# Layer 0's input projection in five chunks of the contraction instead of four

## The chip, the core and the metric

The kernel runs on one core of a Trainium2 chip. The core has a matrix engine (PE, with its weight loads listed as PEld), a vector engine (DVE), an activation engine (ACT), a general engine (POOL), and a queue engine (SP) that issues nearly all transfers from the chip's memory. Each engine takes its own instructions in the order in which they were written into its queue; engines wait for each other by semaphores. Time is the device time of one launch in microseconds (us), lower is better.

## The reference, cut to what matters

Two layers of a bidirectional encoder on x of 256 positions by 2048 channels, all in float32. `c` is one vector of 2048 values.

```python
c_act = silu(c)
for l in range(2):
    shift, scale, gate = split(c_act @ w_ada[l] + b_ada[l], 3)     # w_ada[l]: 2048 x 6144
    h = rmsnorm(x, norm_g[l]) * (1 + scale) + shift                # 256 x 2048
    z = h @ w_in[l]                                                # w_in[l]: 2048 x 6656, 13 pieces of 512
    ...                                                            # four mixers on the 13 pieces:
    # Fourier (f_x, f_g), neighbourhood attention (na_q, na_k, na_v, na_g),
    # retention (r_q, r_k, r_v, r_g), convolution (cv_a, cv_b, cv_g)
    x = x + gate * (concat(o_fft, o_na, o_ret, o_cv) @ w_out[l])   # w_out[l]: 2048 x 2048
out = rmsnorm(x, final_g)
```

So `h` cannot be used before the modulation (shift and scale) of its channels is known, and that takes two thirds of `w_ada[l]`, 33.5 MB in layer 0, read through once. `w_in[l]` is 54.5 MB.

## The kernel before, in words

**Tiles.** The 2048 channels are 16 K tiles of 128. A column of the modulation for one K tile (`Ada`, line 519) is worked out on DVE: a 512 KB half row block of `w_ada` is multiplied by silu(c), spread over all partitions, and summed along the row (line 534). Each K tile takes four of these for layer 0's `h`: shift and scale, two halves each.

**A step of weights** (`Weights`, line 332) is a transfer of two K tiles of one piece of `w_in` (512 KB; one K tile, 256 KB, where a chunk has an odd tail), a split on two engines, and matmuls. The split keeps float32 accuracy with a fast matmul type: ACT writes the rounded high part `whi` (line 351), DVE the rest, `wlo` (line 353). `h` is split the same way into `hh` and `hl`. Each product is then three matmuls: hh·whi, hl·whi, hh·wlo. Pieces that are wanted with channels on the partitions (CVB, CVA, NAQ, NAK, NAG, FGP, CVG) go by lines 370 to 373 with 256 columns each, twelve matmuls per K tile; the others (FXP, NAV, RV, RQ, RK, RG) go by rows, lines 402 to 404 with 512 columns each, six matmuls per K tile. Ten pieces ("first") run in every chunk; RK, CVG and RG ("second") run once at the end over all 16 K tiles.

**Chunks.** In layer 0 the modulation is not there when the kernel starts. The K tiles are therefore cut into chunks, `CH0`, and the ten first pieces run chunk by chunk: while the matmuls of one chunk run, the `Ada` steps for the K tiles of the next chunk are loaded and summed. `merge` (line 1084) spreads these steps evenly between the weight steps of the running chunk, except its last `KEEP` = 4. After three quarters of them comes `prep_x` (line 233): DVE scales x by the reciprocal norm, PE transposes it into a PSUM bank. After the last comes `mod_cols` (line 1115; three small DVE instructions) and `prep_h` (line 282): per K tile two ACT instructions of 128x256 (`hh`, line 296, and the unrounded h, line 301) and a DVE subtraction (`hl`, line 309 or 314). `prep_h` is given a higher place in the order of every engine than the work written around it.

```python
    chunks = first_steps(0, CH0, SEED0)
    steps += mod_chunk(0, *CH0[0])
    for i in range(len(CH0) - 1):
        steps += merge(chunks[i][:-KEEP], mod_chunk(0, *CH0[i + 1])) + chunks[i][-KEEP:]
    tail = chunks[-1] + second_steps(0)
    steps += between(tail, SPAN[0], gates(0, 0) + gates(0, 1) + pair(1, 0))
```

**What a chunk costs beside its matmuls.** A piece has two PSUM banks of the four that are called "acc"; so two pieces are open at most. At the end of each chunk its sum is copied out to an SBUF tile `z` (`done`, line 456; ACT, line 471, 128x512 each, two per piece). In a later chunk the piece is either seeded, that is ACT copies z back into the bank before its first matmul (`seed`, line 437, instruction at line 442) and copies the total out again, or not seeded, and then DVE adds the bank to z (line 473). `SEED0` says for every chunk which of a piece's two banks are seeded. In the first chunk nothing is seeded. The seed of the next piece is issued after the first step of the running one (line 387).

**Order.** `FIRST` (line 1237) has the order of the ten pieces in each chunk. The order differs from chunk to chunk. The last chunk's order is written so that the mixers can start one after another: the convolution's pieces CVB and CVA come first. The mixers' work is cut into small bits which a `Pacer` (line 41) calls after each weight step at fixed rates, so the amount of mixer work that is queued between two weight steps goes by the number of steps, not by time. The tail of layer 0 (last chunk and the three second pieces) also has 48 `Ada` steps spread in it: the gates of layer 0 and the first K tiles of layer 1.

**Loads.** All weight and `Ada` loads go through SP's queue in the order of the steps. There are nine buffers of 512 KB (`RAW`) and, until nine loads ahead of the tail, two more. `whi` and `wlo` have four buffers each (`WB`): the splits may run four steps ahead of the matmuls.

Of the kernel before, what the change touches and what calls it, by code (L numbers as in the profile page):

```python
# [34 lines left out]
FXP, FGP, NAQ, NAK, NAV, NAG, RQ, RK, RV, RG, CVA, CVB, CVG = range(13)  # L35
# [56 lines left out]
def trunk(ctx, tc, x, c, cols, w_ada, w_in, w_fft, na_bias, consts, conv_w_pw, w_out, final_g, out):  # L92
# [322 lines left out]
    def held(w):  # L415

        return w.tags is None and len(ring) >= WB and any(ring[-WB] in u for u in holds)
# [630 lines left out]
    def first_steps(l, chunks, seeds):  # L1048
        groups = {p: Group(l, p, seeds) for p in FIRST[l][0]}
        res = []  # L1050
        for c, (k0, n) in enumerate(chunks):
            ws = []
            order = FIRST[l][min(c, len(FIRST[l]) - 1)]
            for p, after in zip(order, order[1:] + (None,)):
                for k, w in pieces(k0, n):
                    ws.append(Weights(in_src(l, p, k, w), groups[p], k, w, k == k0, k + w == k0 + n))
                    ws[-1].next = groups.get(after)
            res.append(ws)
        return res

    def second_steps(l):
        ws = []
        for p in SECOND[l]:
            g = Group(l, p, (0,))
            for ck in range(4):
                for k in (0, 2):
                    ws.append(Weights(in_src(l, p, 4 * ck + k), g, 4 * ck + k, 2, ck == 0 and k == 0,
                                      ck == 3 and k == 2))
                if p == SECOND[l][-1] and ck < 3:
                    ws.append(Call(o_split(ck)))  # L1070
        return ws
# [12 lines left out]
    def merge(a, b):  # L1084

        n = sum(isinstance(s, Weights) for s in a)
        res, done, i = [], 0, 0
        for s in a:
            res.append(s)
            if isinstance(s, Weights):  # L1090
                i += 1
                while done * n < i * len(b) and done < len(b):
                    res.append(b[done])
                    done += 1
        return res + b[done:]
# [28 lines left out]
    def mod_chunk(l, k0, n):  # L1124
        def done():
            mod_cols(l, k0, n)
            prep_h(l, k0, n)

        if k0 == 0:
            both = [Ada(l, which, k, h) for h in range(2) for k in range(n) for which in range(2)]  # L1130
            both[-1].then = done
            both.insert(2, Call(lambda: spread_c(1)))
            both.insert(4, Call(rms_first))
        else:
            both = mods(l, (0, 1), range(k0, k0 + n), done)
        half = len(both) // 2 if k0 == 0 else 3 * len(both) // 4
        return both[:half] + [Call(lambda: prep_x(l, k0, n))] + both[half:]
# [42 lines left out]
# [6 lines that stand above are left out]
# [27 lines left out]
    for s in steps:  # L1213
        if isinstance(s, Step):
# [3 lines left out]
            while (n_split < min(len(weights), n_w[0] + WB) and pos[id(weights[n_split])] < n_load  # L1218
                   and not held(weights[n_split]) and n_run >= 4 * CH0[0][1]):
                weights[n_split].split()  # L1220
# [8 lines left out]
        if isinstance(s, Weights):  # L1229
# [7 lines left out]
FIRST = (((CVB, FGP, NAQ, CVA, NAK, FXP, NAV, NAG, RV, RQ),  # L1237
          (NAG, NAQ, RQ, NAK, CVB, RV, FXP, FGP, NAV, CVA),
          (RV, NAK, FGP, NAV, NAG, FXP, CVA, NAQ, CVB, RQ),
          (CVB, CVA, NAQ, FXP, NAV, NAG, NAK, FGP, RV, RQ)),  # L1240
         ((NAV, CVA, RV, NAQ, FGP, RQ, NAK, FXP, CVB, NAG),
          (CVB, CVA, NAQ, NAK, NAG, FXP, NAV, RV, FGP, RQ)))
# [3 lines left out]
SECOND = ((RK, CVG, RG), (RK, CVG, RG))  # L1246
LAG = 4
B = (0, 1)
SEED0 = ((), (0, 1), (0, 1), (0, 1))
SEED1 = ((), (0, 1))  # L1250
EVAC = (0, 0)
AHEAD = 100
PACE = {'conv': (2, 1.5), 'na': (0.67, 1), 'fft': (1.75, 2.5), 'ret': (1.25, 1.5)}
CH0 = ((0, 2), (2, 3), (5, 5), (10, 6))
CH1 = ((0, 8), (8, 8))
KEEP = 4
H32A = 2
# [75 lines left out]
```

## Time and profile before

| | |
|---|---|
| median of three runs | 945.87 us (945.86, 945.87, 956.63) |
| the profiled execution, its time | 946.63 us |
| its span, first to last instruction | 944.8 us |
| PE busy | 904.1 us, 96% of the span |
| DVE busy | 774.5 us, 82% |
| ACT busy | 600.4 us, 64% |
| read from memory | 256.61 MB, 274 GB/s over the span |

The page lists groups of instructions as line, engine, operation, output <- inputs, shape, count, then the time that they were busy, the mean of one in ns, and the idle time of the engine just before them with what ended it. A table of windows gives, for each stretch of the span, the busy time of each engine with the number of instructions in it, the clock that PE was granted (1.00 is full), the share of the transfer engines' time that was in use, and GB/s. PE's matmuls overlap their neighbours, so their durations add up to more than the time they take; what one costs is the distance from its start to the next one's start. DVE and ACT instructions overlap by some 0.08 us in the same way.

### The profile page before, as it was taken

Reading aid. Unit: us, or ns where it says so; the run is one execution under the profiler, and the core shown is the slowest. Engines: PE = TensorE matmul, PEld = TensorE weight load, DVE = VectorE, ACT = ScalarE, POOL = GpSimd, SP = SyncE. Lnnn points to the kernel's source line nnn. Section 1 sums busy time; section 2 is a strip of 40 time slices with the busy share of each in tenths; the row PEclk is TensorE's granted clock in tenths of the full one; section 3 lists DMA queues with packets and bytes.
Section 4 is the critical chain, followed back from the end, with each engine's and each line's share of the span. In section 5 each row is a group of like instructions: output and inputs, shape, how many; then the busy total and the mean of one; then the engine's idle time right before and its main releaser. Section 6 shows DMA issues by size and latency. Waiting matters only on the chain.

```text
span 944.8 us, 14744 instructions
## 1 busy us (share of the span) xinstructions
PE 904.1 (96%) x5312; PEld 770.0 (81%) x5312; DVE 774.5 (82%) x1260; ACT 600.4 (64%) x1039; POOL 23.2 (2%) x35
## 2 busy tenths in 40 slices
PE   7789999999999999999999999999999999999995
PEld 3779798898977787788778999999768889788784
DVE  5988989789999999889877897559977967678962
ACT  4478966879877766544645464659889645643541
POOL 1000000000000010000000000000000001010000
PEclk7989999999999999999999999999999999999999
DMA  9999999798797778979966999777755666479922
GB/s 336 398 347 388 368 389 372 255 386 270 248 295 252 248 253 286 327 269 363 326 225 211 341 374 367 222 226 236 228 174 164 199 226 199 140 243 331 326 96 89
DMA packets 109132, 259.68 MB, mean 275 GB/s; under 512 B 8450, under 2 KB 10626, under 8 KB 108804
## 3 DMA queue, kind: packets, MB, share of 16 engines
q1 hardware_dynamic: 108004, 256.11, 78.1%
q0 software_dynamic: 768, 2.11, 0.7%
q8 instruction: 41, 0.67, 0.3%
q10 hardware_dynamic: 288, 0.52, 0.1%
q14 instruction: 31, 0.25, 0.1%
HBM read 256.61 MB, written 2.11 MB: 274 GB/s over the span
## 4 chain that ended last, share of the span: by engine, by line
PE 65%; DVE 15%; DMA 10%; ACT 5%; issue 4%; SPq 0%; POOL 0%; DVEq 0%; POOLq 0%; ACTq 0%
PE acc L402 13%; PE acc L403 13%; PE acc L404 13%; PE acc L370 6%; PE acc L372 6%; PE acc L373 6%; DMA raw<-in_w_ada_dram 5%; DVE wlo L353 5%; DVE raw L534 4%; DMA raw<-in_w_in_dram 4%; PE pwb L791 3%; ACT whi L351 2%; DVE cy L719 1%; DVE cy L703 1%; DMA wsm<-in_w_fft_dram 1%
## 5 line engine op out<-in xcount | busy, mean ns | idle before, releaser
L351 ACT ACTIVATE whi<-raw 128x1024 fp32r<-128x1024 f32 (+1 forms) x272 | 278.0, 1030 | 185.9 <-PE acc L404 81.9
L353 DVE TENSOR_TENSOR wlo<-raw,whi 128x1024 fp32r<-128x1024 f32 (+1 forms) x272 | 320.4, 1183 | 57.6 <-ACT whi L351 54.9
L534 DVE CUSTOM_DVE_ANT_0 raw<-raw,cbc 128x1024 f32<-128x1024 f32 x192 | 233.3, 1221 | 44.7 <-DMA raw<-in_w_ada_dram 44.6
L370 PE MATMUL acc<-hh,whi 128*128 128x256 f32 x896 | 254.6, 285 | 2.3 <-ACT hh L296 1.3
L373 PE MATMUL acc<-hh,wlo 128*128 128x256 f32 x896 | 251.3, 283 | 3.6 <-DVE wlo L353 3.5
L372 PE MATMUL acc<-hl,whi 128*128 128x256 f32 x896 | 252.4, 282 | 1.8 <-DVE hl L309 1.8
L402 PE MATMUL acc<-whi,hh 128*128 128x512 f32 x600 | 241.9, 405 | 5.2 <-ACT z L471 3.5
L403 PE MATMUL acc<-wlo,hh 128*128 128x512 f32 x600 | 239.0, 398 | 1.4 <-DVE wlo L353 1.3
L404 PE MATMUL acc<-whi,hl 128*128 128x512 f32 x600 | 238.2, 397 | 0.0
L370 PEld LDWEIGHTS acc<-hh,whi 128*128 128x128 f32 x896 | 170.3, 190 | 7.7 <-issue 2.8
L373 PEld LDWEIGHTS acc<-hh,wlo 128*128 128x128 f32 x896 | 169.4, 190 | 5.2 <-DVE wlo L353 5.0
L372 PEld LDWEIGHTS acc<-hl,whi 128*128 128x128 f32 x896 | 170.4, 190 | 2.7 <-DVE hl L309 2.1
L402 PEld LDWEIGHTS acc<-whi,hh 128*128 128x128 f32 x600 | 113.2, 189 | 34.8 <-ACT z L471 3.9
L403 PEld LDWEIGHTS acc<-wlo,hh 128*128 128x128 f32 x600 | 113.5, 189 | 28.9 <-DVE wlo L353 4.4
L404 PEld LDWEIGHTS acc<-whi,hl 128*128 128x128 f32 x600 | 113.4, 189 | 27.5 <-issue 1.4
L471 ACT ACTIVATE z<-acc 128x512 f32<-128x512 f32 x108 | 62.2, 599 | 29.7 <-PE acc L373 16.1
L715 ACT ACTIVATE cvp<-uT,constants 128x256 f32<-128x256 f32 x160 | 70.8, 502 | 7.8 <-DVE cy L719 7.8
L719 DVE TENSOR_TENSOR cy<-cy,cvp 128x512 f32<-128x512 f32 x80 | 52.9, 689 | 5.9 <-ACT cvp L715 5.5
L442 ACT ACTIVATE acc<-z 128x512 f32<-128x512 f32 x72 | 41.6, 601 | 0.2
L703 DVE SCALAR_TENSOR_TENSOR cy<-uT,constants,cy 128x256 f32<-128x256 f32 x80 | 34.9, 481 | 0.2
L210 ACT ACTIVATE junk<-xs 128x512 f32<-128x512 f32 x16 | 9.5, 595 | 36.8 <-DVE xs L496 36.8
L495 DVE TENSOR_TENSOR yt<-acc,gate 128x512 f32<-128x512 f32 x16 | 10.5, 685 | 13.6 <-PE acc L404 13.6
(212 smaller groups left out, 710.1 us busy)
## 6 DMA issues: line engine op xcount, KB each, us to landing
raw<-in_w_in_dram SPq DMA_DIRECT2D x198, 512.0 KB, 5.2
raw<-in_w_ada_dram SPq DMA_DIRECT2D x192, 512.0 KB, 6.0
raw<-in_w_out_dram SPq DMA_DIRECT2D x64, 512.0 KB, 5.6
raw<-in_w_in_dram SPq DMA_DIRECT2D x20, 256.0 KB, 7.4
nab<-in_na_bias_dram SPq DMA_DIRECT2D x16, 192.0 KB, 5.0
xs<-in_x_dram SPq DMA_DIRECT2D x2, 1024.0 KB, 6.0
gate<-gate_row POOLq DMA_DIRECT2D x8, 256.0 KB, 5.5
wsm<-in_w_fft_dram SPq DMA_DIRECT2D x4, 512.0 KB, 3.7
```

The lines of the kernel that those rows point to most:

```text
L351: self.on_act = A.activation(self.hi[:, :n], self.raw[:, :n], AF.Copy).ins
L353: self.on_dve = V.tensor_tensor(self.lo[:, :n], self.raw[:, :n], self.hi[:, :n].bitcast(F32), op=ALU.subtract).ins
L370: T.matmul(o, wh[:, sl], hh[:, k], start=fresh and blk % 2 == 0 and blk // 2 not in g.seeded, stop=False, skip_group_check=True)
L372: T.matmul(o, wh[:, sl], hl[:, k], start=False, stop=False, skip_group_check=True)
L373: flags["mm"] = T.matmul(o, wl[:, sl], hh[:, k], start=False, stop=en, skip_group_check=True).ins
L402: T.matmul(o, hh[:, k, sl], wh, start=st, stop=False, skip_group_check=m in g.seeded)
L403: T.matmul(o, hh[:, k, sl], wl, start=False, stop=False, skip_group_check=m in g.seeded)
L404: flags["mm"] = T.matmul(o, hl[:, k, sl], wh, start=False, stop=en, skip_group_check=m in g.seeded).ins
L471: A.activation(o, i, AF.Copy, scale=0.125 if last and self.piece == NAQ else 1.0)
L534: flags["sum"] = V.tensor_tensor_reduce(w, w, cbc[:, self.half * KH:(self.half + 1) * KH], 0.5, 0.0, ALU.mult, ALU.add, to).ins
L715: A.activation(d[:, i], uT[:, b + i, t:t + S], AF.Copy, scale=w[:, t, b + i:b + i + 1])
L719: V.tensor_tensor(y[:, b:b + 2], y[:, b:b + 2], d, op=ALU.add)
```

## The change

Layer 0's 16 K tiles are cut into five chunks of 2, 2, 3, 4 and 5 instead of four of 2, 3, 5 and 6. The new fourth chunk gets an order of the ten pieces of its own; the other orders stay with the first, second, third and last chunk. In the second chunk a piece has its first bank seeded and its second bank added by DVE; in the three later chunks both banks are seeded as before.

```diff
 FIRST = (((CVB, FGP, NAQ, CVA, NAK, FXP, NAV, NAG, RV, RQ),
           (NAG, NAQ, RQ, NAK, CVB, RV, FXP, FGP, NAV, CVA),
           (RV, NAK, FGP, NAV, NAG, FXP, CVA, NAQ, CVB, RQ),
+          (CVB, NAV, NAQ, NAK, RQ, NAG, RV, FXP, FGP, CVA),
           (CVB, CVA, NAQ, FXP, NAV, NAG, NAK, FGP, RV, RQ)),
...
-SEED0 = ((), (0, 1), (0, 1), (0, 1))
+SEED0 = ((), (0,), (0, 1), (0, 1), (0, 1))
...
-CH0 = ((0, 2), (2, 3), (5, 5), (10, 6))
+CH0 = ((0, 2), (2, 2), (4, 3), (7, 4), (11, 5))
```

A pair in `CH0` is (first K tile, number of K tiles). Work by chunk, each with ten pieces; "steps" are weight steps, "sums" the `Ada` steps for the next chunk that are merged into it:

| chunk | before: K tiles, steps, sums | after: K tiles, steps, sums |
|---|---|---|
| 0 | 2, 10, 12 | 2, 10, 8 |
| 1 | 3, 20 (10 of one K tile), 20 | 2, 10, 12 |
| 2 | 5, 30 (10 of one K tile), 24 | 3, 20 (10 of one K tile), 16 |
| 3 | 6, 30 (last chunk) | 4, 20, 20 |
| 4 | | 5, 30 (10 of one K tile; last chunk) |

## The prediction

> **What bounds the kernel now.** I read the page first: its busy times, then the slices of the span (40 of 23.6 us each).
>
> ```profile
> PE 904.1 (96%) x5312; PEld 770.0 (81%) x5312; DVE 774.5 (82%) x1260; ACT 600.4 (64%) x1039; POOL 23.2 (2%) x35
> ...
> PE   7789999999999999999999999999999999999995
> ...
> DVE  5988989789999999889877897559977967678962
> ...
> PEclk7989999999999999999999999999999999999999
> DMA  9999999798797778979966999777755666479922
> ```
>
> PE is the bound of the whole and is short of work only in the first three slices, where the transfers are full and the granted clock dips. DVE is at nine tenths in slices ten to sixteen (212 to 378 us): the tail of layer 0, which is also touched by the change. So I ask two things: what PE loses in the chunks before the tail, and whether the tail can run faster if PE has less to do in it.
>
> The windows come next. A K tile of ten pieces has 96 main matmuls (6 pieces by 12, 4 by 6), so counting them from the first one at 24.77 gives the borders of the chunks; the counts in the rows (198, 299, 493, 673) hold these and the few transposes and mixer matmuls. Rows: chunks 0, 1, 2, 3, then the second pieces up to the place where PE last waits for a split.
>
> ```profile
> 24.77:67.42 42.65, 34.91 (x198) 30.71 (x198) 38.12 (x63) 25.23 (x40) 0.00 (x0) 0.88 1.00 374
> 67.42:114.50 47.08, 44.77 (x299) 40.03 (x298) 42.18 (x69) 41.18 (x71) 0.00 (x0) 1.00 1.01 376
> 114.50:188.72 74.22, 73.47 (x493) 66.55 (x493) 62.18 (x102) 54.24 (x89) 0.00 (x0) 1.00 0.93 340
> 188.72:293.97 105.25, 102.72 (x673) 91.64 (x672) 101.11 (x180) 88.11 (x172) 1.83 (x3) 1.00 0.89 304
> 293.97:340.40 46.43, 44.60 (x253) 34.82 (x252) 44.23 (x97) 33.14 (x67) 1.11 (x2) 1.00 0.67 223
> ```
>
> A matmul's cost is the distance between starts:
>
> ```profile
> 47.38 0.39 PE L404 MATMUL acc<-whi,hl 128*128 128x512 f32 x1
> 47.61 0.39 PE L402 MATMUL acc<-whi,hh 128*128 128x512 f32 x1
> ...
> 59.74 0.28 PE L370 MATMUL acc<-hh,whi 128*128 128x256 f32 x1
> 59.86 0.28 PE L372 MATMUL acc<-hl,whi 128*128 128x256 f32 x1
> ```
>
> That is 0.23 us for 512 columns and 0.12 for 256: 1.4 us for a K tile of one piece (6 x 0.23 or 12 x 0.12), 14.2 us for ten pieces. Chunk 0 should take 28.4 us and takes 42.65; chunk 1 42.6 and takes 47.08; chunk 2 71 and takes 74.22. PE loses 14.3, 4.5 and 3.2 us there, transposes included.
>
> The waits name the losses. First those within chunk 0, then those of PE in chunks 1 and 2.
>
> ```profile
> PE acc L402 <- ACT z L471: 3.5, 1, 3.5
> PE acc L373 <- DVE wlo L353: 2.4, 4, 0.9
> ...
> PE acc L370 <- ACT acc L442: 1.0, 1, 1.0
> PE acc L402 <- ACT acc L442: 0.9, 2, 0.5
> PE acc L402 <- ACT whi L351: 0.7, 1, 0.7
> ```
>
> The 3.5 us is the dearest wait, and the timeline of ACT and DVE around it shows its cause:
>
> ```profile
> 47.05 1.23 DVE L534 CUSTOM_DVE_ANT_0 raw<-raw,cbc 128x1024 f32<-128x1024 f32 x1
> 48.73 0.16 DVE L1121 SCALAR_TENSOR_TENSOR mcol<-mcol,pcol 128x3 f32<-128x3 f32 x1
> 48.99 1.02 ACT L296 ACTIVATE hh<-xt,mcol 128x256 fp32r<-128x256 f32 x2 [0.71 <-DVE mcol L1121]
> 51.25 0.59 ACT L301 ACTIVATE h<-xt,mcol 128x256 f32<-128x256 f32 x1
> 52.65 1.11 ACT L471 ACTIVATE z<-acc 128x512 f32<-128x512 f32 x2
> 53.32 0.80 PE L402 MATMUL acc<-whi,hh 128*128 128x512 f32 x1 [3.51 <-ACT z L471]
> 54.34 0.63 PE L404 MATMUL acc<-whi,hl 128*128 128x512 f32 x1
> 54.77 0.63 PE L402 MATMUL acc<-whi,hh 128*128 128x512 f32 x1
> ...
> 50.00:60.00 10.00, 6.68 (x21) 0.66 1.03 402
> ```
>
> `prep_h` for chunk 1 stands in ACT's queue ahead of the copy that frees PE's banks, and waits for the twelfth sum. When PE resumes, 512 columns cost 0.43 us (54.34 to 54.77); the window from 50 to 60 us has a clock of 0.66, that is 3.4 us lost on top of the 3.5.
>
> [...]
>
> **The change part by part. Chunk 0** has 8 sums merged into its first six steps instead of 12. Transfers are full: at the 402 GB/s of the row above a 512 KB (0.524 MB) load takes 1.30 us. A step with two sums is 3.9 us of transfer against 2.8 of PE; with 1.33 sums it is 3.05. The last sum comes four loads earlier, 5.2 us, near 42 instead of 47.05, and `prep_h` has two K tiles rather than three. ACT is then through with it at about 46, before PE asks for the banks (49.4 before, about 46.5 without the waits for wlo). So 3.5 + 3.4 + 2.4 = 9.3 us are at stake; I take 8 as gained, since 3.05 is still above 2.8, and 4 to 9.3 as bounds.
>
> **One boundary more.** The pieces' sums go out and come back once more.
>
> ```profile
> L471 ACT ACTIVATE z<-acc 128x512 f32<-128x512 f32 x108 | 62.2, 599 | 29.7 <-PE acc L373 16.1 <-PE acc L404 12.6
> L442 ACT ACTIVATE acc<-z 128x512 f32<-128x512 f32 x72 | 41.6, 601 | 0.2
> L495 DVE TENSOR_TENSOR yt<-acc,gate 128x512 f32<-128x512 f32 x16 | 10.5, 685 | 13.6 <-PE acc L404 13.6
> L301 ACT ACTIVATE h<-xt,mcol 128x256 f32<-128x256 f32 x5 | 2.7, 590 | 0.0
> ```
>
> Layer 0 had 80 copies out and 60 seeds. Now it has 90 copies out, 70 seeds and ten DVE additions: 20 x 0.60 = 12 us of ACT, 10 x 0.69 = 6.9 us of DVE (priced by the nearest row, an addition-sized DVE operation from PSUM). They lie beside matmuls, but not freely: in chunk 1 of before ACT was busy 41.18 of 47.08 us. PE waited 2.6 us for seeds and whi in chunks 1 and 2 (the rows above), nearly all of it around chunk 1's `prep_h`: ten ACT instructions of 0.59 less their overlap, some 5 us, against pieces of 4.2. After, three such moments come: 6 instructions (3 us) against pieces of 2.8, 8 (4 us) against 4.2, 10 (5 us) against 5.6. I price them at 2.2, 2.2 and 0.4 us (what is left of the 2.6 for the second such moment now), and the first seed of one more chunk, which nothing hides, at 0.3: 5.1 against 2.6, so +2.5; bounds 0 (the cover holds) and 7 (chunk 1 repeats the old stall, below). The transposes, `prep_x` and the number and bytes of all loads stay the same in sum; the third and fourth chunk break at other K tiles (one more split `hl`, 0.2 us of DVE, covered).
>
> **DVE's feed before the tail.** DVE starts are 1.15 us apart for a sum, 1.14 for a full split, 0.61 for a half:
>
> ```profile
> 92.27 1.22 DVE L534 CUSTOM_DVE_ANT_0 raw<-raw,cbc 128x1024 f32<-128x1024 f32 x1
> 93.42 1.22 DVE L534 CUSTOM_DVE_ANT_0 raw<-raw,cbc 128x1024 f32<-128x1024 f32 x1
> ...
> 94.56 0.69 DVE L353 TENSOR_TENSOR wlo<-raw,whi 128x512 fp32r<-128x512 f32 x1
> 95.17 1.22 DVE L534 CUSTOM_DVE_ANT_0 raw<-raw,cbc 128x1024 f32<-128x1024 f32 x1
> ...
> 60.42 1.23 DVE L353 TENSOR_TENSOR wlo<-raw,whi 128x1024 fp32r<-128x1024 f32 x1 [1.04 <-ACT whi L351]
> ```
>
> With 3 to 4 us of preparation per chunk and half the additions in each of chunks 1 and 2: chunk 1, 12 x 1.15 + 10 x 1.14 + 6 = 31 us against 28.4 of PE; chunk 2, 16 x 1.15 + 10 x 1.75 + 7 = 43 against 42.6; chunk 3, 20 x 1.15 + 20 x 1.14 + 7 = 53 against 56.8. The excess of chunk 1 is covered by DVE's lead: the first split of that chunk ended at 61.65 (last row), 5.8 us ahead of PE. If that cover is gone it costs up to 2.6. I put it at nothing.
>
> So the tail begins at 188.7 + 14.2 (one more K tile ahead of it) - 8 + 2.5 = 197.4, 8.7 us later.
>
> **The tail** loses the same 14.2 us of PE. But DVE sees only ten half splits less, 10 x 0.53 = 5.3 us; the mixers' bits, 30 + 24 steps and 48 sums are unchanged. Up to 340.40 DVE is busy 101.11 + 44.23 = 145.3 of 151.7 us, 95.8%. After, 140.0 us of DVE must go through. At 95.8% that takes 146.1 us, 5.6 less than now; with DVE never idle 11.7 less. Who waits for whom there:
>
> ```profile
> PE pwb L791 <- DMA wsm<-in_w_fft_dram: 1.7, 1, 1.7
> PE nas L815 <- ACT napt L851: 0.7, 1, 0.7
> ...
> PE acc L373 <- DVE wlo L353: 1.1, 1, 1.1
> ```
>
> In the last chunk PE never waits for a split (first two rows); in the second pieces it does once, for 1.1 us (third row). So DVE now builds a lead which it uses up behind it; part of its idle time is time in which it was ahead, and that it can give. I take 97.5%: 143.6 us, 8.1 less. What is late next is wlo, for which PE will wait at the end of the last chunk and in the second pieces.
>
> **Sum.** +8.7 - 8.1 = +0.6 on the span of 944.8, with 1.8 us around it (946.63). That execution stands 0.8 above the median of 945.87; the forecast on the median's footing is 946.5, which I round to 946: what the first boundary gives, the added boundary and DVE in the tail take back.
>
> **Rivals.** *The tail gives nearly all back.* DVE's queue holds the sums for gates and for layer 1, which nobody needs soon, and fills its idle time: 11.7 off the tail instead of 8.1, and the boundary priced at its lower bound, 0 instead of 2.5: 946.5 - 6.1 = 940. For it: PE had no wait for DVE in the last chunk. Against: DVE at 101.11 of 105.25 with the queue in order. With the full 9.3 in chunk 0 too it is 939.
>
> *The old stall comes back in chunk 1* (slower). Chunk 1 of after has just the shape of chunk 0 of before: ten steps, 12 sums in the first six, `prep_h` of three K tiles ahead of the copies in ACT's queue, and seeds besides. It decides if DVE ends the twelfth sum after PE has finished the sixth step, that is, if the lead of 5.8 us is spent by then: six steps with two sums and a split want 3.44 us of DVE and 3.9 of transfer each against 2.8, 3.6 to 6.6 us in all. Then PE loses 3.5 + 3.4 + 2.4 = 9.3 there instead of 2.2, +7.1: 953.6. Against: fewer sums in chunk 0 let the loads and DVE run further ahead.
>
> [...]
>
> *The tail gives nothing.* DVE and ACT (88.11 of 105.25 in the last chunk) stop each other as often as now, and the mixers' bits, which go by steps and not by time, keep it at 95.8% or below with the waits moved to PE: the tail shortens by 3 instead of 8.1, 951.6.
>
> **Chances.** Forecast 0.5 (942 to 950 as its own range), tail gives back 0.2, old stall in chunk 1 0.2, tail gives nothing 0.1. The range takes in the rivals of both sides and the bounds of chunk 0's gain (4 instead of 8): 936 to 956. A measurement of this kernel tells about 2% from no change; that is under 927 or over 965. The whole loss before the tail is 22 us, of which some 15 would have to go for the first, so 0.02; two of the slower cases would have to meet, with the clock dropped in each, for the second, 0.04.
>
> **What would show it.** Right: no wait of PE for `z` at line 471 in chunk 0 over 1 us, a clock of 1.00 from 45 to 60 us, chunk 1 beginning near 59; PE's waits for line 442 one place more; the tail's start near 197 in the span; from there to the second pieces DVE at 97% or more with PE waiting for wlo at line 353 several us in all. Wrong: a clock below 0.9 after 60 us (old stall), a tail start over 201, or a tail in which PE waits for no split although it is 14 us shorter.

## The result: 1.1% slower, outside the range

The changed kernel takes 958.80 us (median of 958.32, 958.80 and 959.91) against 945.87: a ratio of 1.0114, 95% interval 1.008 to 1.0148. The prediction was 946, no change, with a range of 936 to 956. The profiled execution took 959.91 us with a span of 957.9, against 946.63 and 944.8. (The medians of the kernel before on the chips of the experiments lie at 948 to 951 us, so runs are compared by their ratio to it on the same chip. One run's profiled execution, e12's, was disturbed and is not read.)

The page of the changed kernel, busy times and slices as before:

```profile
PE 908.1 (95%) x5312; PEld 771.5 (81%) x5312; DVE 781.4 (82%) x1274; ACT 609.9 (64%) x1059; POOL 24.6 (3%) x35
...
PE   6897989999989999999999999999999999999996
...
DVE  5999778889997999898878798559977967667962
...
PEclk7999999999989999999999999999999999999998
```

Same instructions on PE, 20 more on ACT. The first slices have a cleaner clock than before, but PE is short of work in more places, and DVE is no fuller in the tail (slices ten to sixteen) than it was.

The windows by chunk, borders counted in the same way: chunks 0 to 4, then the second pieces up to the last wait for a split.

```profile
24.72:58.41 33.69, 29.95 (x199) 26.81 (x197) 31.71 (x48) 23.66 (x36) 0.00 (x0) 1.00 1.04 398
58.41:94.14 35.73, 30.82 (x200) 27.93 (x199) 34.35 (x56) 25.56 (x39) 0.00 (x0) 0.95 0.97 357
94.14:142.03 47.89, 45.20 (x298) 41.48 (x297) 37.06 (x57) 39.77 (x68) 0.00 (x0) 0.96 0.91 324
142.03:202.49 60.46, 58.48 (x396) 53.31 (x395) 51.95 (x89) 46.59 (x77) 0.00 (x0) 1.00 0.92 337
202.49:300.90 98.41, 92.60 (x575) 81.11 (x573) 93.33 (x173) 80.01 (x161) 1.83 (x3) 0.97 0.81 277
300.90:351.10 50.20, 47.38 (x255) 34.82 (x254) 46.16 (x100) 36.59 (x77) 1.10 (x2) 1.00 0.71 237
```

Chunk 0 is 9.0 us shorter. Chunk 1 takes 35.7 us for 28.4 of matmuls, chunk 2 47.9 for 42.6, chunk 3 60.5 for 56.8: 16.3 us lost behind chunk 0, where it was 7.7. The tail starts at 202.5, 13.8 us later than before. Its last chunk takes 98.4 us where the old one less 14.2 would be 91.

The waits of PE, in the order of the same windows (one row of chunk 0, two of chunk 1, one each of chunks 2, 3 and 4, two of the second pieces):

```profile
PE acc L402 <- ACT z L471: 1.0, 1, 1.0
...
PE acc L402 <- ACT acc L442: 3.0, 1, 3.0
PE acc L402 <- DVE z L473: 1.9, 1, 1.9
...
PE acc L370 <- ACT whi L351: 2.2, 1, 2.2
...
PE acc L373 <- DVE wlo L353: 1.8, 2, 1.3
...
PE acc L402 <- ACT whi L351: 4.5, 1, 4.5
...
PE acc L403 <- DVE wlo L353: 0.9, 2, 0.5
PE acc L373 <- DVE wlo L353: 0.8, 1, 0.8
```

The stall of the old chunk 0 is now in chunk 1. The timeline there, DVE, ACT and PE:

```profile
74.52 1.22 DVE L534 CUSTOM_DVE_ANT_0 raw<-raw,cbc 128x1024 f32<-128x1024 f32 x1
...
76.44 1.02 ACT L296 ACTIVATE hh<-xt,mcol 128x256 fp32r<-128x256 f32 x2 [3.59 <-DVE mcol L1121]
...
78.69 0.58 ACT L301 ACTIVATE h<-xt,mcol 128x256 f32<-128x256 f32 x1
79.14 2.02 ACT L351 ACTIVATE whi<-raw 128x1024 fp32r<-128x1024 f32 x2
81.03 0.62 ACT L442 ACTIVATE acc<-z 128x512 f32<-128x512 f32 x1
...
78.23 0.47 PE L402 MATMUL acc<-whi,hh 128*128 128x512 f32 x1 [1.90 <-DVE z L473]
81.71 0.79 PE L402 MATMUL acc<-whi,hh 128*128 128x512 f32 x1 [3.01 <-ACT acc L442]
82.30 0.63 PE L403 MATMUL acc<-wlo,hh 128*128 128x512 f32 x1
82.73 0.63 PE L404 MATMUL acc<-whi,hl 128*128 128x512 f32 x1
```

ACT stands still for 3.59 us with the preparation of K tiles 4 to 6 at the head of its queue; the splits and the seed that PE needs come out of it at 79.14 and 81.03. The clock is at 0.50 from 81.13 to 84.55 (0.95 in the window); from 81.71 on, where PE resumes, that costs another 1.4 us.

Two sums by part, changed kernel against before:

| part | forecast | measured, profiled executions |
|---|---|---|
| chunk 0 | -8 | -9.0 (33.7 against 42.7) |
| one more K tile ahead of the tail | +14.2 | +14.2 (in the chunks' own lengths) |
| losses in the other chunks ahead of the tail | +2.5 | +8.6 (16.3 against 7.7) |
| tail, to the start of the last second piece (RG) | -8.1 | -3.0 (170.3 against 173.3) |
| from there to the end | 0 | +2.4 (585.2 against 582.8) |
| sum | +0.6 | +13.2 |

Within the tail the last chunk gives 6.8 of the 14.2 us back (98.4 against 105.3), and the second pieces up to RG take 3.8 us longer (71.8 against 68.0).

### The profile page after: what moved, and what is told of

The parts are those of the page before. It is cut to its first block, busy times and chain, and to the rows that moved or that the text cites. A ratio compares the mean times of both kernels' runs of the same rounds, so it can differ in the third digit from the quotient of the medians.

```text
span 957.9 us, 14773 instructions
## 1 busy us (share of the span) xinstructions
PE 908.1 (95%) x5312; PEld 771.5 (81%) x5312; DVE 781.4 (82%) x1274; ACT 609.9 (64%) x1059; POOL 24.6 (3%) x35
## 4 chain that ended last, share of the span: by engine, by line
PE 60%; DVE 18%; DMA 11%; ACT 5%; issue 5%; POOL 0%; SPq 0%; DVEq 0%; POOLq 0%; ACTq 0%
PE acc L404 10%; PE acc L402 10%; PE acc L403 10%; PE acc L373 7%; PE acc L370 7%; PE acc L372 7%; DMA raw<-in_w_ada_dram 7%; DVE wlo L353 6%; DVE raw L534 5%; DMA raw<-in_w_in_dram 3%; PE pwb L791 2%; DMA raw<-in_w_out_dram 2%; ACT whi L351 1%; DVE cy L703 1%; DVE cy L719 1%
## 5 line engine op out<-in xcount | busy, mean ns | idle before, releaser
L353 DVE TENSOR_TENSOR wlo<-raw,whi 128x1024 fp32r<-128x1024 f32 (+1 forms) x272 | 319.8, 1181 | 60.8 <-ACT whi L351 54.2
L534 DVE CUSTOM_DVE_ANT_0 raw<-raw,cbc 128x1024 f32<-128x1024 f32 x192 | 232.8, 1219 | 44.8 <-DMA raw<-in_w_ada_dram 44.7
L372 PEld LDWEIGHTS acc<-hl,whi 128*128 128x128 f32 x896 | 170.4, 190 | 2.5 <-DVE hl L309 1.8
L471 ACT ACTIVATE z<-acc 128x512 f32<-128x512 f32 x117 | 67.1, 596 | 30.5 <-PE acc L404 15.7
L442 ACT ACTIVATE acc<-z 128x512 f32<-128x512 f32 x81 | 46.9, 600 | 0.6 <-DVE uT L473 0.2
```

Source lines behind the costliest of these rows:

```text
L353: self.on_dve = V.tensor_tensor(self.lo[:, :n], self.raw[:, :n], self.hi[:, :n].bitcast(F32), op=ALU.subtract).ins
L372: T.matmul(o, wh[:, sl], hl[:, k], start=False, stop=False, skip_group_check=True)
L471: A.activation(o, i, AF.Copy, scale=0.125 if last and self.piece == NAQ else 1.0)
L534: flags["sum"] = V.tensor_tensor_reduce(w, w, cbc[:, self.half * KH:(self.half + 1) * KH], 0.5, 0.0, ALU.mult, ALU.add, to).ins
```

## The experiments

Each row: the ratio to the kernel before on the same chip, and from the profiled execution the length of the chunks, the start of the tail and the tail's length up to RG, in us. Borders are counted as above. In the last row the ratio is e12's, the rest e13's, which is the same kernel.

| run | ratio (95%) | chunks | tail starts | tail |
|---|---|---|---|---|
| before | 1 | 42.7, 47.1, 74.2, then 105.3 | 188.7 | 173.3 |
| changed | 1.0114 (1.008 to 1.0148) | 33.7, 35.7, 47.9, 60.5, then 98.4 | 202.5 | 170.3 |
| e1: 2, 2, 3, 3, 6 | 1.0117 (1.0086 to 1.0148) | 34.5, 36.5, 43.0, 58.1, then 106.8 | 197.0 | 174.1 |
| e2: 2, 3, 6, 5 | 1.0129 (1.0091 to 1.0166) | 40.5, 53.0, 87.5, then 95.5 | 207.7 | 167.3 |
| e3: changed, light gates | 0.9949 (0.9924 to 0.9974) | 33.8, 37.2, 46.4, 60.4, then 88.6 | 203.1 | 152.3 |
| e4: before, light gates | 1.0014 (0.9993 to 1.0034) | 41.4, 47.1, 74.2, then 101.5 | 187.4 | 165.7 |
| e5: before, chunk 0 spread | 0.992 (0.9891 to 0.995) | 34.8, 49.0, 74.2, then 105.5 | 182.5 | 173.6 |
| e6: changed, chunk 1 spread | 0.9992 (0.997 to 1.0015) | 34.1, 29.8, 45.0, 60.8, then 96.3 | 194.6 | 168.1 |
| e7: changed, light sums in chunk 1 | 1.0037 (1.0014 to 1.0059) | 32.8, 35.2, 44.7, 60.8, then 96.6 | 199.4 | 168.6 |
| e8: changed, both banks seeded | 1.0091 (1.006 to 1.0122) | 32.3, 35.9, 45.5, 60.5, then 95.0 | 200.1 | 166.7 |
| e9: before, all spread | 0.9993 (0.9965 to 1.002) | 33.6, 44.4, 82.0, then 111.3 | 186.1 | 178.7 |
| e10: changed, all spread | 1.0136 (1.0095 to 1.0177) | 29.5, 32.3, 45.8, 68.1, then 97.9 | 202.0 | 170.4 |
| e11: changed, late preparation | 1.0087 (1.0054 to 1.012) | 32.8, 36.1, 47.9, 60.5, then 98.4 | 203.1 | 170.4 |
| e12, e13: changed, preparation behind | 1.0034 (1.0015 to 1.0053) | 33.8, 31.1, 44.7, 60.8, then 96.3 | 195.3 | 168.5 |

### The boundary and the shorter tail, one at a time

```diff
-CH0 = ((0, 2), (2, 2), (4, 3), (7, 4), (11, 5))
+CH0 = ((0, 2), (2, 2), (4, 3), (7, 3), (10, 6))
```

> The changed kernel with the last chunk left at 6 K tiles: chunks 2, 2, 3, 3, 6. It has the added boundary but moves no matmul out of the tail. Theory (the tail of layer 0 is paced by DVE and its loads, so that matmuls taken out of it are hardly got back; the boundary pays for itself by the 9 us that chunk 0 gains): the tail starts at 187 to 191 us, as before, and takes as long as before; 944 to 949 us in all. Rival (the added boundary itself, with its copies, seeds and additions, costs the 13 us): 956 to 960 us.

```diff
-CH0 = ((0, 2), (2, 3), (5, 5), (10, 6))
+CH0 = ((0, 2), (2, 3), (5, 6), (11, 5))
```

> The kernel before with one K tile moved from the last chunk to the one ahead of it: four chunks 2, 3, 6, 5. No added boundary. Theory: the tail starts 14 to 16 us later (near 203) and its last chunk takes 97 to 101 us, not the 91 that PE would need; 954 to 959 us. Rival (the boundary costs, the tail gives its time back): 944 to 948 us.

Each half costs as much as the whole. e2's last chunk took 95.5 us, less than the theory's 97 to 101 and more than 91, and its tail starts 19 us later (2 of them lie ahead of chunk 0), not 14 to 16. e1 went against the theory: its tail is the old one, but starts at 197, and the time is in the rival's range. The two windows in which they lose most, e1's chunk 3 and e2's chunk 1:

```profile
138.80:197.00 58.20, 48.25 (x302) 42.74 (x301) 50.92 (x94) 45.03 (x81) 0.00 (x0) 0.94 0.94 349
...
67.20:120.20 53.00, 46.87 (x302) 41.05 (x301) 47.91 (x77) 43.77 (x75) 0.00 (x0) 0.97 1.02 383
```

Both chunks have three K tiles, 42.6 us of matmuls, and carry the sums for six. Their weights are 3 K tiles for each of ten pieces at 0.262 MB (7.9 MB), and the sums want 24 rows of 0.524 MB (12.6 MB), 20.4 MB in all. At the 383 GB/s of the second row this is 53.3 us, the length of e2's chunk 1, whose transfers are full (a share of 1.02). In e1's chunk 3 they are full only up to 168 us (399 to 408 GB/s, then 301 and 287); behind that PE waits for seeds (3.2 us in the chunk), and ACT is never idle from 182 us on. A chunk of n K tiles ahead of one of m moves 2.62 n + 2.10 m MB. At about 400 GB/s, the best that a chunk's window shows, matmuls of 14.2 n us cover that up to m/n of about 1.46. This is an estimate and no sharp limit, since loads brought in ahead help a chunk over it: before has ratios of 1.5, 1.67 and 1.2, and in e9 (below) the chunk at 1.67 took 44.4 us for 42.6 of matmuls. The changed kernel has 1, 1.5, 1.33 and 1.25. e1 and e2 have a chunk at 2, which I had not priced, so neither is a clean test of the boundary or of the tail.

### Is the tail paced by DVE

```diff
-                flags["sum"] = V.tensor_tensor_reduce(w, w, ..., 0.5, 0.0, ALU.mult, ALU.add, to).ins
+                if self.l == 0 and self.which == 2:
+                    flags["sum"] = V.tensor_scalar(to, w[:, 0:1], 0.5, 0.0, op0=ALU.mult, op1=ALU.add).ins
+                else:
+                    flags["sum"] = V.tensor_tensor_reduce(w, w, ..., 0.5, 0.0, ALU.mult, ALU.add, to).ins
```

> The changed kernel with the 32 sums for layer 0's gates left out of DVE (their rows are loaded as before, and one column of each is copied by a small DVE instruction in place of the sum over 1024 columns; layer 0's gate is wrong by it). That takes 32 x 1.15 = 37 us from DVE in the tail and nothing from PE, ACT or the loads. Theory: PE becomes the bound there, the last chunk takes 91 to 94 us instead of 98.4, PE's waits for whi and wlo in the second pieces go; 945 to 951 us. Rival (the tail is not paced by DVE): 956 to 960 us, as the changed kernel.

> The kernel before with the same 32 sums left out (layer 0's gate is wrong by it). Theory: PE hardly waits for DVE in that tail now, so little is gained: 941 to 946 us; and the changed kernel with the same sums left out is then at most 5 us slower than this one, where with the sums it is 13 slower. Rival (the difference lies at the boundaries ahead of the tail): both get the same amount and stay 13 us apart.

The windows of the last chunk and of the second pieces up to RG, the changed kernel's first, then that of before:

```profile
203.10:291.60 88.50, 88.24 (x577) 79.09 (x577) 74.17 (x162) 84.01 (x175) 1.83 (x3) 1.00 0.92 324
291.60:355.40 63.80, 63.20 (x418) 52.47 (x417) 62.40 (x124) 47.12 (x100) 2.39 (x3) 1.00 0.88 307
```

```profile
187.40:288.90 101.50, 101.50 (x674) 91.81 (x673) 86.44 (x180) 94.82 (x189) 1.83 (x3) 1.00 0.95 336
288.90:353.10 64.20, 63.58 (x418) 52.38 (x416) 59.51 (x114) 43.44 (x89) 2.56 (x3) 1.00 0.86 300
```

With 32 of its sums gone, the changed kernel's tail is 18 us shorter (152.3 against 170.3) and now 13.4 us shorter than that of before with the same cut: of the 14.2 us of matmuls taken out of the tail, nearly all come back. In the kernels as they are 3.0 did. PE is the bound (88.24 of 88.50), and the 13 us between the two kernels turn into 3 the other way by the medians (945.5 against 948.6), 6 by the ratios. So DVE's sums pace the tail. e3 went as the theory said, its last chunk (88.6 us) even under the 91 to 94. e4 missed its range: its tail is 7.6 us shorter, but its time is 948.6 and not 941 to 946. What the runs don't part is DVE's time and the load buffers, which DVE's sums free: with fewer sums the loads flow faster too (324 against 277 GB/s).

### What stalls PE in chunk 1

```diff
-        steps += merge(chunks[i][:-KEEP], mod_chunk(0, *CH0[i + 1])) + chunks[i][-KEEP:]
+        steps += merge(chunks[i][:-KEEP[i]], mod_chunk(0, *CH0[i + 1])) + chunks[i][-KEEP[i]:]
...
-KEEP = 4
+KEEP = (1, 4, 4)
```

> The kernel before, with the 12 sums merged into the first nine of chunk 0's ten steps instead of the first six; nothing else. Theory (what stalls PE at a boundary is that the sums for the next chunk, and with them the preparation in ACT's queue, are packed ahead of splits and copies that PE needs sooner): chunk 0 takes 34 to 38 us instead of 42.7, the tail starts 4 to 8 us earlier; 937 to 942 us. Rival (the transfers, full until 165 us, set the start of the tail): chunk 0 gets shorter, chunks 1 and 2 longer by as much, the tail starts at 187 to 190 us as before; 944 to 947 us.

The same for the changed kernel, with `KEEP = (4, 1, 4, 4)`:

> The changed kernel, with the 12 sums in chunk 1 merged into its first nine steps instead of the first six; nothing else. Theory: the old stall in chunk 1 goes, 30 to 32 us instead of 35.7, and the time falls by 3 to 6 us, to 953 to 956. Rival (the transfers): chunk 1 shorter, chunks 2 and 3 longer; 957 to 960 us.

The window of e5's chunk 0, and of e6's chunk 1:

```profile
24.60:59.40 34.80, 31.27 (x199) 28.51 (x200) 33.39 (x53) 24.50 (x38) 0.00 (x0) 0.95 1.04 399
```

```profile
58.90:88.70 29.80, 28.99 (x199) 26.79 (x197) 28.80 (x45) 23.17 (x38) 0.00 (x0) 1.00 0.98 371
```

Both stalls go, 7.9 us in chunk 0 of before and 5.9 in chunk 1 of the changed kernel, and most of the gain reaches the end. e5 is faster than both kernels: 941.02 us, a ratio of 0.992. The changed kernel with its stall mended is level with before (0.9992; its time fell by more than the 3 to 6 us expected; chunk 2 got shorter too, 45.0 against 47.9, and the tail, 168.1 against 170.3).

Three causes were left: DVE late with the sums, the loads packed into six steps, or the place of the preparation. e7 took the 12 sums off DVE:

```diff
+                if self.l == 0 and self.which < 2 and 4 <= self.k < 7:
+                    flags["sum"] = V.tensor_scalar(to, w[:, 0:1], 0.5, 0.0, op0=ALU.mult, op1=ALU.add).ins
```

> The changed kernel with the 12 sums for K tiles 4 to 6, which are merged into chunk 1, left out of DVE (the rows are loaded as before, one column of each is copied; shift and scale of these K tiles are wrong by it). 14 us less of DVE in chunk 1, the loads as they are. If the stall in chunk 1 is DVE's lateness with the sums: chunk 1 takes 28.5 to 30.5 us, its waits for line 442 and 473 go, the clock stays at 1.00. If it is the transfers: 34 us or more.

Its chunk 1, and what ACT waited for in it:

```profile
58.70:93.90 35.20, 32.20 (x200) 28.83 (x200) 25.66 (x43) 25.38 (x39) 0.00 (x0) 0.90 0.99 365
```

```profile
ACT hh L296 <- PE xt L251: 2.8, 1, 2.8
```

DVE is 8.7 us less busy, and the chunk takes 35.2 us all the same. By the line that I had drawn that speaks for the loads, but the wait names a third thing: the preparation now waits 2.8 us in ACT's queue for PE's transposes instead of for the sums. So DVE's lateness is not needed for the stall. e11 was to tell place from loads by writing the preparation three steps later:

```diff
-            both = mods(l, (0, 1), range(k0, k0 + n), done)
+            both = mods(l, (0, 1), range(k0, k0 + n), None if k0 == 4 else done)
+            late[k0] = Call(done)
...
+        steps += chunks[i][-KEEP:-1] + ([late[4]] if i == 1 else []) + chunks[i][-1:]
```

> The changed kernel with all loads and sums where they are (12 sums in the first six steps of chunk 1), but the preparation of K tiles 4 to 6 written three steps later, after the ninth step of chunk 1. If the stall in chunk 1 comes from the place of the preparation in ACT's queue, ahead of splits, copies and seeds: chunk 1 takes 29.5 to 31.5 us, as with the sums spread over nine steps, and the whole is at 949 to 954 us. If it comes from the packing of the loads: chunk 1 stays at 34 us or more and the whole at 956 to 960.

It tells nothing: the preparation's higher place in the order pulled it forward again, its first instruction to the same place in ACT's queue and the rest one split behind it. Chunk 1 takes 36.1 us with the same waits. In e12 it has no higher place:

```diff
-        with tc.high_priority(offset=AHEAD):
+        with tc.issue_after(flags["mm"]) if l == 0 and k0 == 4 else tc.high_priority(offset=AHEAD):
             prep_h_(l, k0, n)
```

> The changed kernel with all loads and sums in their old order, and the preparation of K tiles 4 to 6 behind in ACT's and DVE's queues: in the run with the late preparation alone its higher place had pulled it back to where it was, so here it has no higher place. One of its six ACT instructions stays ahead in ACT's queue (and waits some 3.6 us there), five go behind the splits, copies and seeds of the next four steps. If the queue's order makes the stall in chunk 1: PE's wait for line 442 falls from 3.0 to under 1 us, the clock stays at 1.00 and chunk 1 takes 30.5 to 33 us instead of 35.7; chunk 2 may get longer, since it gets its tiles later. If the loads make it: chunk 1 stays at 35 us or more with the same waits.

> The same kernel as the run before, for its timeline, since that run's profiled execution was a disturbed one. The time (ratio 1.0034 to the kernel before, against 1.0114 of the changed kernel) already speaks for the queue's order. If that is so: chunk 1 takes 30.5 to 33 us, PE waits under 1 us for line 442 there, and transfers and sums land at the same times as in the changed kernel (the last sum for K tiles 4 to 6 at 75 to 76 us). If chunk 1 is 35 us or more, the gain came from later chunks and the stall stays unexplained.

The ratio is 1.0034, and e13 has the timeline: the window of its chunk 1, PE's waits (the first in chunk 1, the second in chunk 2), and the start of the last sum with ACT's wait.

```profile
58.60:89.70 31.10, 29.20 (x199) 26.90 (x199) 29.82 (x47) 24.23 (x38) 0.00 (x0) 1.00 1.00 374
```

```profile
PE acc L402 <- DVE z L473: 1.9, 1, 1.9
PE acc L402 <- ACT acc L442: 0.9, 1, 0.9
```

```profile
74.70 1.22 DVE L534 CUSTOM_DVE_ANT_0 raw<-raw,cbc 128x1024 f32<-128x1024 f32 x1
...
76.62 0.56 ACT L296 ACTIVATE hh<-xt,mcol 128x256 fp32r<-128x256 f32 x1 [3.59 <-DVE mcol L1121]
77.08 1.04 ACT L351 ACTIVATE whi<-raw 128x1024 fp32r<-128x1024 f32 x1
78.03 0.59 ACT L442 ACTIVATE acc<-z 128x512 f32<-128x512 f32 x1
```

The last sum starts at 74.70, as in the changed kernel (74.52), and the loads go out in the same order within 0.2 us of the same times. Five ACT instructions moved behind splits and seeds, and DVE's subtractions of the preparation with them: the seed comes at 78.03 instead of 81.03, PE's wait for it in chunk 1 (3.0 us) is gone, the clock stays at 1.00 and chunk 1 takes 31.1 us. Chunk 2 doesn't pay for it; it is 3.2 us shorter. The intervals of the two ratios, 1.0015 to 1.0053 and 1.008 to 1.0148, don't meet. So the place of the preparation in the queues makes the greater part of the stall, ACT's above all, since the wait that went is one for ACT; the packing of the loads doesn't. The 1.9 us for line 473 stay, and they are DVE's own: it reaches that addition at 77.58, behind the last two sums and a split, without a pause.

### Smaller parts, and spreading everywhere

```diff
-SEED0 = ((), (0,), (0, 1), (0, 1), (0, 1))
+SEED0 = ((), (0, 1), (0, 1), (0, 1), (0, 1))
```

> The changed kernel with both banks seeded in chunk 1 as in all later chunks: ten more seeds on ACT there, ten additions fewer on DVE. Theory: this part of the change is small, within 2 us of the changed kernel either way (956 to 960): DVE gets 6.9 us back in the chunk where it is late, ACT gets 6 us more behind the preparation. Rival (the additions are what makes chunk 1 late, PE waited 1.9 us for line 473): chunk 1 takes 31 to 33 us instead of 35.7 and the whole is 3 to 5 us faster.

Chunk 1 takes 35.9 us and PE's waits in it become one of 4.7 us for line 442: the ten additions are not what makes chunk 1 late. The whole is at 1.0091, an interval that overlaps that of the changed kernel.

`KEEP = (1, 1, 1)` in the kernel before, and `(1, 1, 1, 1)` in the changed one:

> The kernel before with the sums of chunks 0, 1 and 2 each merged into all steps but the last one. Theory (the place of the preparation): chunk 1 of five-tile preparations also gets shorter than the 49 us that it takes when only chunk 0 is spread, by 1 to 3 us; 938 to 942 us. Rival (chunk 1 is held by the transfers, which are full in it): no further gain, 941 to 944 us.

> The changed kernel with the sums of chunks 0 to 3 each merged into all steps but the last one. Theory: one or two us less than with chunk 1 alone spread, 945 to 949 us, still behind four chunks with the same spreading by 5 to 9 us, since the tail gives only some 6 of the 14 us of matmuls back. Rival (five chunks are the better cut once the boundaries are clean): 935 to 941 us.

Both theories missed. Spreading the sums of the later chunks moves the preparation so near to the end that the next chunk has to wait for it: e9's chunk 1 gets shorter (44.4 us), its chunk 2 takes 82.0 instead of 74.2, with a wait of 4.2 us for a seed at its end; e10's chunk 3 takes 68.1 instead of 60.5, with one of 4.8. So the spread paid in chunk 0 of before, in chunk 1 of the changed kernel and in e9's chunk of three K tiles, and lost more in the chunks of five (e9) and four (e10), which prepare six and five K tiles.

## Why the prediction was wrong

**Chunk 0** was right in mechanism and size: 9.0 us where 8 was taken, PE's wait for z at 1.0 us, a clock of 1.00, chunk 1 beginning at 58.4 for "near 59".

**One boundary more** is the first step that failed: "the first seed ... +2.5; bounds 0 ... and 7", measured 8.6, beyond the bound. I had named the case as a rival with its price (9.3 instead of 2.2; measured 7.3 lost in chunk 1), and gave it 0.2 because DVE's lead would be "spent by then" only if loads and sums fell behind. That was the wrong condition. e7 has the sums early and stalls, e13 has them late and loses 2.7 us in place of 7.3. The preparation stood at the head of ACT's queue, which is served in order (the seed of chunk 1 came at 81.03 behind it and at 78.03 ahead of most of it), ahead of the splits, copies and seeds of the next pieces, and in a chunk of two K tiles a piece gives only 2.8 us of cover. DVE's own part, the wait for line 473, was 1.9 of the 7.3. The same step was written at the same place in a chunk of the same shape: that should have made the stall the forecast and not the rival. Chunk 2 lost 5.3 us and chunk 3 3.7; with chunk 1 mended by queue order chunk 2 loses 2.1. But e7, whose chunk 1 takes as long as the changed kernel's, loses 2.1 in chunk 2 as well, so it isn't shown that the stall itself was handed down. Two of my signs of being wrong came: a clock of 0.83 from 80 to 90 us and a tail start of 202.5. What is left in chunk 3 was not traced; with this cut and the old spread in that chunk it takes 60.4 to 60.8 us in every run.

**The tail** is the second: "I take 97.5%: 143.6 us, 8.1 less", measured 3.0. What held is that DVE's sums pace the tail (e3). What did not is the size, and DVE's work at a steady share was the wrong way to get it. DVE ran at (93.33 + 46.16) / 148.6 = 93.9%, below even the 95.8% of before. Most of what the last chunk lost sits in one place, and PE doesn't wait there for DVE's wlo, as I had said, but for a split whose load was late; SP, POOL, DVE, ACT and PE in turn:

```profile
270.39 0.38 SPq L327 DMA_DIRECT2D raw<-in_w_in_dram  x1
272.73 1.53 SPq L125 DMA_DIRECT2D wsm<-in_w_fft_dram  x2
...
270.27 1.08 POOL L571 DMA_DIRECT2D gate<-gate_row  x2 [4.47 <-DMA gate_row<-gcol]
...
270.28 0.08 DVE L534 DVE_READ_ACCUMULATOR2_ANT msum<- 128x1 f32 x1
...
279.25 1.06 ACT L351 ACTIVATE whi<-raw 128x1024 fp32r<-128x1024 f32 x1 [4.07 <-DMA raw<-in_w_in_dram]
...
280.36 1.22 PE L402 MATMUL acc<-whi,hh 128*128 128x512 f32 x2 [4.54 <-ACT whi L351]
```

DVE's sum frees a buffer at 270.36, SP issues the weight load at once, and the load lands only at 279.23, 8.8 us later (the median of its kind from 240 to 285 us is 6.3). ACT splits it at 279.25, and PE stands for 4.5 us. The clock is at 0.50 from 279.1 to 285.9, and from 280.36 on, where PE resumes, that costs another 2.8: together 7.3 of the 9.8 us that this chunk is longer than e3's (98.4 against 88.6). The same load took 8.2 us in the kernel before, out at 262.24 and split at 270.46, and PE's only wait around it was 1.7 us for a load of the Fourier mixer. In e3, with 32 sums fewer, it went out at 258.36, 12 us earlier, and its split at 270.10 waits for nothing. In all three the gate's transfers from POOL and two loads for the Fourier mixer go out within 8 us of it; whether they slow it was not tried. That chain is read from the timeline; no run took it apart.

**Independence.** I treated "old stall in chunk 1" and "tail gives nothing" as alternatives, with 0.2 and 0.1. They are two mechanisms at two places, and both happened. Their prices added, 946.5 + 7.1 + 5.1 = 958.7, meet the measured 958.8; that this is so near is luck, since the rival in chunk 1 was priced at 9.3 us and lost 7.3, chunk 0 gained 1.0 more than forecast, and 2.4 came behind the tail. The range left that case out.

**After the tail** 0 was forecast, and the profiled execution shows +2.4 us, in the output projections of both layers (93.7 against 92.8 us, 102.2 against 100.0). That execution is 1.1 us over the median of its kernel. The same stretch, 585.2 us here and 582.8 before, lies between 583.0 and 586.0 in all experiments read but e3 and e4, so +2.4 is within what it varies by.

## What to carry to other kernels

When a schedule gives a step a higher place, ask what stands behind it in its engine's queue and for how long it will wait there itself: here five short ACT instructions made a chunk 4.6 us longer. Moving them took the changed kernel from a ratio of 1.0114 to 1.0034, and spreading the work ahead of them in the first chunk alone made the kernel before 0.8% faster, which the new cut did not. Work taken from a stage need not shorten it as long as something else paces the stage (here 14.2 us of matmuls gave 3.0 back, and 13.4 with 32 of DVE's sums gone): cut the pacing engine's work in a trial first, and see whether the stage follows. A share of busy time does not give the price of a stage when the loss is one late load (here 8.8 us, for which PE stood 4.5); look for who waits for it and what covers it. And where chunks carry the loads for the next one, work out from bytes and matmul time by how much a chunk may grow (here an estimate of 1.46): the two chunks at 2 lost 15.6 and 10.4 us.

## What the runs showed of the hardware

The granted clock was at 0.50 around gaps of PE shorter than the 3.51 us one in chunk 0 of the kernel before. In chunk 1 of e7 PE was idle for 2.42 us, and behind that 512 columns cost 0.43 us (80.99 to 81.42) where they cost 0.23 at a clock of 1.00. PE's rows, and the windows of this stretch:

```profile
79.05 0.77 PE L402 MATMUL acc<-whi,hh 128*128 128x512 f32 x1 [2.42 <-DVE z L473]
...
80.99 0.63 PE L403 MATMUL acc<-wlo,hh 128*128 128x512 f32 x1
81.42 0.63 PE L404 MATMUL acc<-whi,hl 128*128 128x512 f32 x1
...
78.70:82.10 3.40, 2.47 (x5) 1.71 (x6) 3.40 (x6) 3.40 (x6) 0.00 (x0) 0.50 1.02 382
82.10:85.50 3.40, 3.40 (x10) 2.63 (x10) 3.36 (x6) 0.80 (x3) 0.00 (x0) 0.50 0.98 339
```

In chunk 2 of the changed kernel a wait of 2.18 us for a split, up to 131.22, and one of 0.52 up to 132.48 go with a clock of 0.50 from 132.35 to 135.76, while one of 1.91 us in chunk 1 of e13 goes with none (1.00 in the window). In chunk 1 of the changed kernel there are two gaps, 1.90 and 3.01 us up to 78.23 and 81.71, with one matmul between them, and one stretch at 0.50, from 81.13 to 84.55. So the stretches at 0.50 lasted 3.4 us in these two chunks and 6.8 in e7 (78.70 to 85.50) and in the last chunk of the changed kernel (279.1 to 285.9, around the gap of 4.54 us). What decides whether the clock drops, and for how long, no run here shows.

Taking 37 us of DVE work (32 sums, whose starts lie 1.15 us apart) out of the tail of the kernel before (e4) made its tail 7.6 us shorter and its time no shorter (1.0014): as much was lost in layer 0's output projection, 100.8 us instead of 92.8. Which queue gives it back there was not looked into.
